# A two-layer backbone on one core: where the second attention's values, the output projection's weights and the last sums stand in the order

## The chip, the cores and the metric

The kernel runs on one core of a Trainium2 chip. A core has five engines with a queue of instructions each, and every queue runs in its order: TensorE (PE in the profile, with PEld for its weight loads), VectorE (DVE), ScalarE (ACT), GpSimd (POOL) and SyncE (SP), which starts most of the DMA transfers. Matmuls write to PSUM, which is divided into banks of 128 x 512 fp32. The metric is the time of one execution on the device in microseconds (us), as the median of several runs.

## The reference

512 latent tokens (`x`) and 256 context tokens (`ctx`) of width 1024 go through two layers, in fp32. Each layer is a mixer (an attention with its projections) and a SwiGLU FFN, both behind an RMSNorm with a shift and scale from a conditioning vector and followed by a gated residual. The heart of it:

```python
hx = _rms(x, norm_mix_w[l]) * (1.0 + scx1) + shx1          # same for ctx
if l % 2 == 0:   # 8 heads of windowed attention with a sink, 8 of dense attention, head size 64
    ax, ac = _even_mixer(hx, hc, ...)
else:            # 8 differential heads: two score maps of head size 64 on values of 128
    ax, ac = _odd_mixer(hx, hc, ...)
x = x + gx1 * ax
x = x + gx2 * _swiglu(_rms(x, norm_ffn_w[l]) * (1.0 + scx2) + shx2, ffn_w_in[l], ffn_w_out[l])
# ctx likewise, except in the last layer

def _diff_attend(q, k, v, lam):          # layer 1, one block of queries
    s = einsum('bqhad,bkhad->bhaqk', q, k) * scale
    p = softmax(s)
    a = p[:, :, 0] - lam * p[:, :, 1]
    return einsum('bhqk,bkhe->bqhe', a, v)      # then RMSNorm per head, then @ w_out

def _swiglu(h, w_in, w_out):             # hidden size 2816
    gate, up = split(h @ w_in)
    return (silu(gate) * up) @ w_out
```

## The kernel before

**Numbers.** Every large product is made of three matmuls on operands split in a high and a low part (`hi` is the value rounded by a copy on ACT, `lo` the rest by a subtraction): hi x hi, hi x lo and lo x hi. A weight takes this path too. `unit` starts a DMA into a raw tile, then ACT casts the high part (line 320, `woh`, `wgh`, `wuh` and so on) and either DVE (line 324) or POOL in four pieces (`sub_by_pool`, line 310) subtracts the low part (`wol`, `wgl`, ...).

**Tiles.** Tokens are in tiles of 128: 0 to 3 are latent, 4 and 5 context. The normalized input of a projection is kept transposed (`hT` for latent, `hTc` for context tokens, each hi and lo); a norm writes it by transposes on PE (`npt`, line 287), a scale and shift on ACT and DVE (lines 292 and 294) and a split (296 and 297). The sum of squares of a norm is taken on ACT (279), its inverse root on POOL (147, 148, then 281).

**Order.** Most of the order is not written out by hand: a scheduler walks the program, simulates it and puts each engine's instructions into one queue, by the order in which they are written, their priority (`tc.high_priority`) and when it holds their operands to be ready. Waits on a buffer come from pools: a tile with a tag gets one of the tag's buffers and waits until their last readers are done. A chip that is slower or faster than the simulation waits, but keeps the order.

**Layer 1's attention.** For head h of 8 and query tile t of 4 (line 1034), `attend1` makes scores (`sc`, 661 and 662), the maximum on DVE (664), exponentials on ACT (666), the difference of the two maps on DVE (673); then, behind a `yield`, transposes (`ppt`, 680), copies (`PT`, 683 and 685), the values (`av`, 688) and the norm per head (690 to 695). `Staggered` runs a step's first part, and then the rest of the step before it: values follow one step's scores. Queries and keys of the next head (`inps`, lines 421 to 423) come from a generator that `emit` advances between steps: a copy (`qkv`, 619), squares (`sq`, 375) and their sum (`qss`, 377), the inverse root (`rs_q`, 147 and 148), the scaled result (`qy`, 622), its split (`qd`, `kd`, 627 to 631), transposes (`qpt` 640, `kpt` 646) and their copies (`qt` 642, `kT` 647).

**Output projection.** `out_units` makes its eight weight K-tiles (tag `whi`/`wlo`, four buffers in each of two pools), for layer 1 with the third raw room `wor`. `OutProj.operand` writes a tile of attention results transposed into the place of `hT` (in layer 1 by transposes `opt`, then 728 and 729), `OutProj.sums` runs over the two halves n of 512 columns, and in each over the eight K-tiles (`ops`, 738 to 740), with the residual behind each half (`residual`: 428 multiplies by the gate, 429 adds). In layer 1 the weights are made at head 7, tile 0, and tiles 0 to 2 are projected between the steps of head 7; tile 3 and the four norms follow.

**FFN.** In eleven passes of two column blocks of 128, `pg` and `pu` (line 771) are gate and up sums in two PSUM tiles of the scores' pool `p_sc` (2 x 2 banks). Weights `wg`, `wu` use the same four buffers as the projection's weights. In the first pass the first block runs over two segments of tokens, so that it can start before all norms are there. The down sums (`dps`, 809 to 811) are made of one or two passes at once: nj = 2 blocks, or 4 at the end, where they take turns in two banks.

The lines around which the change works:

```python
ps = acc_tile("dps")                      # nj > 2: two banks, in turn
...
tag=("acc0", "tr0", "acc1", "tr1")[turn["sum"]]       # else: four banks
...
def push(self, gen):                      # Staggered
    next(gen)
    self.flush()
    self.last = gen
```

## Time and profile before

| | |
|---|---|
| median of 3 runs | 1806.88 us (1805.52 to 1808.76) |
| the profiled execution | 1809.33 us, span 1807.5 us |
| mean granted clock of TensorE | 0.986 |
| busy: PE, DVE, ACT, POOL | 1725.7, 995.7, 807.5, 618.6 us |
| moved by DMA | 165.65 MB, 92 GB/s |

The page lists for each engine how long it worked. A line of the waits says which instruction stood idle, and which other engine's instruction released it. A line of the timeline has the start, the length, the engine, the source line and the result's and operands' names; in square brackets how long the engine had been idle before, and what ended that. A granted clock of 0.50 means that TensorE ran at half its speed in that stretch.

The program's stages by time: layer 0's attention up to about 430 us, its FFN to 1020, the first projections of layer 1 to 1065, its attention to 1371, the rest of the output projection to 1419, the FFN to the end.

### The profile page before, as it was taken

What the parts mean: (1) busy time and instruction counts of PE and PEld (TensorE: products, weight loads), DVE (VectorE), ACT (ScalarE), POOL (GpSimd) and SP (SyncE); (2) the same over time, 40 slices, a digit from 0 to 9 for tenths busy, and PEclk for the clock granted to TensorE, in tenths of its full rate; (3) what the DMA queues carried; (4) which work ended last, traced back from release to release, by engine and by line L of the source; (5) the groups of instructions that cost most, each with busy time, mean ns of one, the idle gap of its engine ahead of it and who ended that gap; (6) DMA issues with size and microseconds to landing.
All of it is one profiled execution on the core that took longest, in us unless ns stands there. A gap on an engine that the chain in (4) does not pass through costs nothing. (4 is left out here: it accounts for less than half of the span.)

```text
span 1807.5 us, 26161 instructions
## 1 busy us (share of the span) xinstructions
PE 1725.7 (95%) x9910; PEld 1459.7 (81%) x9910; DVE 995.7 (55%) x1737; ACT 807.5 (45%) x1710; POOL 618.6 (34%) x944
## 2 busy tenths in 40 slices
PE   6899999889999999999999999999988999999998
PEld 4887787667888888888888889999977788888886
DVE  4665555435265465655552656666663556655653
ACT  6556556434264343333332566666663422232230
POOL 2763334322064344332322577776653100000000
PEclk8999999999999999999999999999999899999999
DMA  9212234203452334344331211111122233233231
GB/s 309 55 44 75 78 96 138 71 26 110 155 164 83 98 101 152 117 129 136 111 98 33 79 42 47 45 45 36 33 82 70 82 105 105 70 112 98 71 116 47
DMA packets 152478, 165.65 MB, mean 92 GB/s; under 512 B 16480, under 2 KB 139936, under 8 KB 152352
## 3 DMA queue, kind: packets, MB, share of 16 engines
q1 hardware_dynamic: 152000, 163.77, 29.1%
q8 instruction: 78, 1.28, 0.3%
q14 instruction: 48, 0.39, 0.1%
q10 hardware_dynamic: 352, 0.21, 0.0%
HBM read 159.73 MB, written 4.22 MB: 91 GB/s over the span
## 5 line engine op out<-in xcount | busy, mean ns | idle before, releaser
L771 PE MATMUL pg<-hT,wgh 128*128 128x512 f32 (+1 forms) x720 | 244.2, 391 | 0.8 <-DVE hT L297 0.7
L771 PE MATMUL pu<-hT,wuh 128*128 128x512 f32 (+1 forms) x720 | 243.6, 390 | 1.3 <-ACT wuh L320 1.3
L428 DVE TENSOR_TENSOR dps<-dps,g 128x512 f32<-128x512 f32 x200 | 136.2, 696 | 106.6 <-PE dps L811 99.3
L809 PE MATMUL dps<-wdh,hdh 128*128 128x512 f32 x440 | 175.9, 401 | 3.8 <-DVE x L429 3.5
L810 PE MATMUL dps<-wdl,hdh 128*128 128x512 f32 x440 | 174.1, 396 | 0.0
L811 PE MATMUL dps<-wdh,hdl 128*128 128x512 f32 x440 | 165.4, 395 | 0.0
L771 PEld LDWEIGHTS pg<-hT,wgh 128*128 128x128 f32 x720 | 135.3, 189 | 31.6 <-DVE hT L297 1.3
L771 PEld LDWEIGHTS pu<-hT,wuh 128*128 128x128 f32 x720 | 135.2, 189 | 31.0 <-ACT wuh L320 1.5
L771 PE MATMUL pu<-hT,wul 128*128 128x512 f32 (+1 forms) x360 | 140.4, 390 | 0.8 <-DVE wul L324 0.8
L771 PE MATMUL pg<-hT,wgl 128*128 128x512 f32 (+1 forms) x360 | 140.4, 390 | 0.0
L421 PE MATMUL inps<-wih,hT 128*128 128x384 f32 x384 | 133.2, 347 | 2.7 <-ACT qkv L619 2.7
L429 DVE TENSOR_TENSOR x<-x,dps 128x512 f32<-128x512 f32 x200 | 132.8, 683 | 3.3
L422 PE MATMUL inps<-wil,hT 128*128 128x384 f32 x384 | 130.6, 340 | 0.0
L423 PE MATMUL inps<-wih,hT 128*128 128x384 f32 x384 | 130.3, 339 | 0.0
L310 POOL TENSOR_TENSOR wil<-wir,wih 128x256 fp32r<-128x256 f32 x132 | 104.1, 817 | 69.7 <-ACT wih L320 69.1
L201 ACT ACTIVATE modw<-modw,cols 128x256 f32<-128x256 f32 x192 | 82.2, 498 | 82.8 <-DMA modw<-in_mod_w_dram 80.7
L434 ACT CAST hdh<-pu 128x768 fp32r<-128x768 f32 (+1 forms) x44 | 30.4, 691 | 177.6 <-DVE pu L787 177.6
L809 PEld LDWEIGHTS dps<-wdh,hdh 128*128 128x128 f32 x440 | 82.7, 188 | 26.0 <-DVE x L429 4.3
L771 PE MATMUL pg<-hTc,wgh 128*128 128x256 f32 x352 | 99.4, 286 | 2.3 <-ACT hTc L296 2.1
L811 PEld LDWEIGHTS dps<-wdh,hdl 128*128 128x128 f32 x440 | 82.3, 188 | 19.7
L771 PE MATMUL pu<-hTc,wuh 128*128 128x256 f32 x352 | 98.0, 282 | 0.0
L810 PEld LDWEIGHTS dps<-wdl,hdh 128*128 128x128 f32 x440 | 82.8, 188 | 17.9
(237 smaller groups left out, 4187.5 us busy)
## 6 DMA issues: line engine op xcount, KB each, us to landing
modw<-in_mod_w_dram SPq DMA_DIRECT2D x96, 512.0 KB, 4.9
wgr<-in_ffn_w_in_dram SPq DMA_DIRECT2D x44, 512.0 KB, 3.5
wur<-in_ffn_w_in_dram SPq DMA_DIRECT2D x44, 512.0 KB, 3.5
wdr<-in_ffn_w_out_dram SPq DMA_DIRECT2D x44, 512.0 KB, 3.5
wir<-in_od_w_in_dram SPq DMA_DIRECT2D x96, 128.0 KB, 2.3
x<-in_x_dram SPq DMA_DIRECT2D x8, 512.0 KB, 4.7
wir<-in_ev_w_in_dram SPq DMA_DIRECT2D x16, 256.0 KB, 3.0
wor<-in_ev_w_out_dram SPq DMA_DIRECT2D x8, 512.0 KB, 3.6
```

Source lines behind the costliest of these rows:

```text
L201: nc.scalar.activation(pr[:, k], w[:, k], AF.Copy, scale=cols[:, kk:kk + 1])
L310: nc.gpsimd.tensor_sub(lo[c], raw[c], hi[c])
L421: nc.tensor.matmul(ps, hs[0][:, k, :], a, start=k == 0, stop=False)
L422: nc.tensor.matmul(ps, hs[0][:, k, :], b, start=False, stop=False)
L423: nc.tensor.matmul(ps, hs[1][:, k, :], a, start=False, stop=k == KT - 1)
L428: nc.vector.tensor_mul(tmp, ps, g[:, n * 512:(n + 1) * 512])
L429: eng.tensor_add(xt[:, n * 512:(n + 1) * 512], xt[:, n * 512:(n + 1) * 512], tmp)
L434: nc.scalar.copy(hi, src)
L771: nc.tensor.matmul(ps[:, s0:s1], a, cols_T(b, s0, s1)[:, k, :], start=k == 0 and q == 0, stop=k == KT - 1 and q == 2)
L809: nc.tensor.matmul(ps, hh, a, start=j == 0, stop=False)
L810: nc.tensor.matmul(ps, hh, b, start=False, stop=False)
L811: nc.tensor.matmul(ps, hl, a, start=False, stop=j == nj - 1)
```

## The change

1. `Staggered` has a depth, in layer 1 two: values follow two steps' scores. `PBUF`, the buffers of the transposed probabilities, goes from 4 to 6. At the end the norms, the remaining values and the projection of tiles 2 and 3 are interleaved.
2. The weights of the output projections are made by `OutProj.weights` inside `behind_marks`: the last `qd` and `kd` and the last exponential on each engine are marked as they are written, and the weights are issued behind these. In layer 1 they begin at head 7, tile 1 instead of tile 0; in layer 0 three at block 3, tile 0 and the rest at tile 1.
3. `last_sums` makes the sums of the last projected tile (5 in layer 0, 3 in layer 1) K-tile by K-tile, both halves n in a tile of two banks, instead of half by half.
4. In layer 1's FFN `pg` and `pu` share one tile of two banks (`pgu`); the first pass runs both column blocks over two segments: 192 matmuls of 256 columns in place of 96 of 256 and 48 of 512.
5. The last down sums of layer 1 take turns in four banks, those of layer 0 do so for the first four sums.
6. `rt` is made by another form of instruction, 32 times.

```diff
-PBUF = 4
+PBUF = 6
...
+    def behind_marks():
+        stack = ExitStack()
+        for ins in marks.values():
+            stack.enter_context(tc.issue_after(ins))
+        return stack
...
-                nc.vector.tensor_sub(qd[:, 1], yb, f32(qd[:, 0]))
+                mark(nc.vector.tensor_sub(qd[:, 1], yb, f32(qd[:, 0])))
...
-            nc.scalar.copy(kd[:, :, 0, :], y[:, nq:nq + 2])
-            nc.gpsimd.tensor_sub(kd[:, :, 1, :], y[:, nq:nq + 2], f32(kd[:, :, 0, :]))
+            mark(nc.scalar.copy(kd[:, :, 0, :], y[:, nq:nq + 2]))
+            mark(nc.gpsimd.tensor_sub(kd[:, :, 1, :], y[:, nq:nq + 2], f32(kd[:, :, 0, :])))
...
+        def weights(self, n=KT):
+            with behind_marks():
+                self.ws.extend(w for _, w in zip(range(n), self.units))
...
+        def last_sums(self, t):
+            ohi, olo = tile_T(0, t), tile_T(1, t)
+            ps = p_sc.tile([P, 1024], F32, name="ops", tag="sc")
+            for k in range(KT):
+                for x, j, q in ((ohi, 0, 0), (ohi, 1, 1), (olo, 0, 2)):
+                    for n in range(2):
+                        c = slice(n * 512, (n + 1) * 512)
+                        nc.tensor.matmul(ps[:, c], x[:, k, :], self.ws[k][j][:, c],
+                                         start=k == 0 and q == 0, stop=k == KT - 1 and q == 2)
+            for n in range(2):
+                residual(self.xs[t], ps[:, n * 512:(n + 1) * 512], self.g[0 if t < NTX else 1], n)
...
+            def places():
+                if ntok > NTX:
+                    return [p_sc.tile([P, 1024], F32, name=name, tag="sc")[:, :n_tok] for name in ("pg", "pu")]
+                both = p_sc.tile([P, 1024], F32, name="pgu", tag="sc")
+                return both[:, :SEQ], both[:, SEQ:]
+
+            ps = []
+            if p == 0 and ntok == NTX:
+                ps = [places() for j in range(2)]
+                for s in first_segs:
+                    for j in range(2):
+                        for w, z in zip((wg, wu), ps[j]):
+                            half(j, w, z, [[s]])
...
+            sums = 0
...
-                    if nj > 2:
+                    sums += 1
+                    if nj > 2 and ntok > NTX and sums > 4:
                         ps = acc_tile("dps")
...
+                if b == 3 and t == 0:
+                    oproj.weights(3)
+                if b == 3 and t == 1 and hp == 0:
+                    oproj.weights()
...
-    for t in range(5, NT):
-        oproj.operand(t)
-        oproj.sums(t)
+    oproj.operand(5)
+    oproj.last_sums(5)
...
-            if h == 7 and t == 0:
+            if h == 7 and t == 1:
...
-            if h == 7 and 0 < t <= 3:
-                oproj.operand(t - 1)
+                oproj.weights()
+            if h == 7 and t >= 2:
+                oproj.operand(t - 2)
...
-                    oproj.sums(t - 1, 0, opa.pool, nc.gpsimd)
+                    oproj.sums(t - 2, 0, opa.pool, nc.gpsimd)
...
-    att.flush()
-    for t in range(3, NTX):
-        oproj.operand(t)
-        oproj.sums(t)
...
+    norm1(0)
+    att.pop()
+    oproj.operand(2)
+    with tc.high_priority(-1000):
+        oproj.sums(2, 0, opa.pool, nc.gpsimd)
+    norm1(1)
+    att.pop()
+    oproj.operand(3)
+    norm1(2)
+    oproj.last_sums(3)
+    norm1(3)
```

What this moves in the queues, at three places. Where lines above the change were added, the same statement has a higher line number after it (320 becomes 331, 310 becomes 321).

ACT in layer 1's attention, from the copy of the last projected query and key tile on. Before, `woh` are the casts of the first two weights, `sq` to `kd` the last query tile's chain:

```order
L619 COPY qkv<-inps 128x384
L320 CAST woh<-wor 128x1024 x2
L375 ACTIVATE sq<-qkv 128x256
L647 CAST kT<-kpt 128x2x128
L690 ACTIVATE o_9810<-av,rc 128x128
L642 CAST qt<-qpt 128x512
L693 ACTIVATE o_14027,oss<-o_9810 128x128
L627 CAST qd<-qy 128x256
L630 CAST kd<-qy 128x2x64
```

After:

```order
L630 COPY qkv<-inps 128x384
L386 ACTIVATE sq<-qkv 128x256
L658 CAST kT<-kpt 128x2x128
L701 ACTIVATE o_9808<-av,rc 128x128
L653 CAST qt<-qpt 128x512
L704 ACTIVATE o_13999,oss<-o_9808 128x128
L638 CAST qd<-qy 128x256
L641 CAST kd<-qy 128x2x64
L331 CAST woh<-wor 128x1024 x2
L658 CAST kT<-kpt 128x2x128
L653 CAST qt<-qpt 128x512
```

The two casts moved from behind `qkv` to behind the last `kd`, ahead of the copies of that tile's transposes.

POOL at the same place; before, `wol` is the first weight's subtraction in four pieces:

```order
L620 COPY vv<-qkv 128x128
L310 TENSOR_TENSOR wol<-wor,woh 128x256 x4
L147 TENSOR_SCALAR rs_o<-oss 128x1
L147 TENSOR_SCALAR rs_q<-qss 128x4
L148 TENSOR_TENSOR rs_o<-rs_o,neghalf 128x1
L148 TENSOR_TENSOR rs_q<-rs_q,neghalf 128x4
L622 TENSOR_TENSOR qy<-qy,rs_q 128x256
L631 TENSOR_TENSOR kd<-qy,kd 128x2x64
```

After:

```order
L631 COPY vv<-qkv 128x128
L158 TENSOR_SCALAR rs_q<-qss 128x4
L159 TENSOR_TENSOR rs_q<-rs_q,neghalf 128x4
L158 TENSOR_SCALAR rs_o<-oss 128x1
L633 TENSOR_TENSOR qy<-qy,rs_q 128x256
L159 TENSOR_TENSOR rs_o<-rs_o,neghalf 128x1
L642 TENSOR_TENSOR kd<-qy,kd 128x2x64
L321 TENSOR_TENSOR wol<-wor,woh 128x256 x8
```

The pieces moved from behind `vv` to behind `kd`, and are those of two weights there.

PE at the seam of the layers, around the transposes of the last latent tile's norm (`npt`) and of keys (`kpt`). Before:

```order
L287 MATMUL npt<-cst,nh 128x128 x8
L421 MATMUL inps<-wih,hT_110 128x384
L422 MATMUL inps<-wil,hT_110 128x384
L423 MATMUL inps<-wih,hT_111 128x384
L421 MATMUL inps<-wih,hT_110 128x384
L422 MATMUL inps<-wil,hT_110 128x384
L423 MATMUL inps<-wih,hT_111 128x384
L421 MATMUL inps<-wih,hTc_4716 128x256
L422 MATMUL inps<-wil,hTc_4716 128x256
L423 MATMUL inps<-wih,hTc_4717 128x256
L421 MATMUL inps<-wih,hTc_4716 128x256
L422 MATMUL inps<-wil,hTc_4716 128x256
```

After:

```order
L434 MATMUL inps<-wih,hT_111 128x384
L432 MATMUL inps<-wih,hT_110 128x384
L433 MATMUL inps<-wil,hT_110 128x384
L434 MATMUL inps<-wih,hT_111 128x384
L298 MATMUL npt<-cst,nh 128x128 x8
L657 MATMUL kpt<-identr,kd 128x128 x4
L432 MATMUL inps<-wih,hT_110 128x384
```

The twelve `inps` matmuls that stood between `npt` and `kpt` now stand ahead of `npt`.

## The prediction

> **What bounds the kernel now.** I read the page first, then the busy time by stage, then what TensorE waited for in the one stage where it is not busy, and last the order of time on each engine there.

> ```profile
> PE 1725.7 (95%) x9910; PEld 1459.7 (81%) x9910; DVE 995.7 (55%) x1737; ACT 807.5 (45%) x1710; POOL 618.6 (34%) x944
> ```

> TensorE (PE) is the bound: 1807.5 - 1725.7 = 81.8 us of idle time are all that a new order can win, besides time at a low granted clock. No other engine is near that. The stretches around the change, where the columns are the length, the busy time of PE, its weight loads, DVE, ACT and POOL, then the granted clock and the DMA share:

> ```profile
> 1065.00:1330.00 265.00, 258.73 (x1794) 247.69 (x1794) 176.40 (x349) 170.78 (x445) 175.13 (x314) 1.00 0.13 38
> 1330.00:1342.00 12.00, 5.14 (x30) 4.44 (x29) 4.34 (x8) 6.22 (x14) 8.35 (x13) 0.78 0.44 132
> 1342.00:1371.00 29.00, 24.05 (x133) 19.67 (x132) 21.55 (x34) 17.03 (x37) 12.94 (x18) 0.86 0.45 146
> 1371.00:1419.00 48.00, 47.18 (x235) 38.32 (x234) 15.65 (x27) 15.72 (x33) 15.40 (x21) 1.00 0.04 12
> 1419.00:1440.00 21.00, 17.47 (x105) 16.06 (x104) 14.51 (x24) 12.81 (x22) 1.85 (x3) 0.76 0.58 174
> 1440.00:1780.00 340.00, 340.00 (x1467) 273.73 (x1466) 192.19 (x246) 86.47 (x103) 0.00 (x0) 1.00 0.29 90
> ```

> The heads of layer 1 (265 us) lose 6.3 us, spread out. The attention's end and the weights of the output projection (1330 to 1371) lose 6.9 + 4.9 us, the projection itself 0.8, the start of layer 1's FFN 3.5. From 1440 to 1780 PE never stops: nothing to win there. The waits of PE from 1330 to 1440:

> ```profile
> PE qpt L640 <- ACT qd L627: 6.5, 1, 6.5
> PE ops L738 <- ACT hT L728: 2.5, 1, 2.5
> PE pu L771 <- ACT wuh L320: 1.3, 1, 1.3
> PE pu L771 <- DVE wul L324: 0.8, 1, 0.8
> PE npt L287 <- POOL nroom L281: 0.7, 1, 0.7
> PE pg L771 <- DVE hT L297: 0.7, 1, 0.7
> ```

> **The clock** costs time on top of the idle:

> ```profile
> 1364.00:1367.40 3.40, 2.35 (x7) 1.97 (x8) 3.12 (x7) 0.53 (x2) 1.66 (x2) 0.50 0.50 152
> ...
> 1422.00:1425.40 3.40, 1.62 (x11) 1.42 (x12) 1.96 (x3) 3.40 (x6) 0.76 (x3) 1.00 0.50 130
> 1425.40:1428.80 3.40, 2.71 (x13) 2.27 (x12) 3.05 (x4) 3.06 (x7) 1.09 (x1) 0.50 0.50 154
> 1428.80:1432.20 3.40, 2.73 (x13) 2.58 (x13) 2.56 (x6) 1.78 (x4) 0.00 (x0) 0.50 0.48 162
> 1432.20:1435.60 3.40, 3.40 (x18) 3.34 (x18) 1.87 (x3) 1.68 (x4) 0.00 (x0) 0.50 0.68 203
> ...
> 1029.50:1033.00 3.50, 2.53 (x18) 2.20 (x16) 2.29 (x6) 3.07 (x8) 0.00 (x0) 1.00 0.00 0
> ```

> A stretch of 3.4 us in which PE was busy for 1.62 us (48%) is followed by a clock of 0.50; one with 2.53 of 3.50 (72%) kept the full clock. At 0.50 half the busy time is lost: behind 1425.4 that is (2.71 + 2.73 + 3.40) / 2 = 4.4 us.

> **Weights behind the attention (layer 1).** In the order of time on ACT, POOL and ACT again:

> ```profile
> 1329.61 2.00 ACT L320 CAST woh<-wor 128x1024 fp32r<-128x1024 f32 x2
> 1331.51 0.42 ACT L375 ACTIVATE sq<-qkv 128x256 f32<-128x256 f32 x1
> ...
> 1330.74 3.94 POOL L310 TENSOR_TENSOR wol<-wor,woh 128x256 fp32r<-128x256 f32 x4 [0.42 <-ACT woh L320]
> 1335.83 1.01 POOL L148 TENSOR_TENSOR rs_q<-rs_q,neghalf 128x4 f32<-128x4 f32 x1
> 1336.92 0.61 POOL L622 TENSOR_TENSOR qy<-qy,rs_q 128x256 f32<-128x256 f32 x1
> ...
> 1337.56 0.40 ACT L627 CAST qd<-qy 128x256 fp32r<-128x256 f32 x1 [4.32 <-POOL qy L622]
> ...
> 1359.73 2.94 ACT L320 CAST woh<-wor 128x1024 fp32r<-128x1024 f32 x3 [1.17 <-DMA wor<-in_od_w_out_dram]
> ```

> The last query tile's normalization stands behind two weight casts (2.00) on ACT and one weight's subtraction (3.94) on POOL, and PE's 6.52 us is that queue. The change puts both behind. Then sq starts at 1329.6, when the casts do now, and about 4.5 us later (0.42, DVE's sum, 1.01, 0.61 and the gaps between) qd: PE can go on near 1334.5 instead of 1338.0, 3.5 us sooner. But the two casts now stand between kd and the copies of kT and qt, so the transposes behind those come only some 2.4 us sooner. What is late next are the weights: their last three casts waited for a DMA until 1359.73, and what a K-tile needs of POOL or DVE comes after that. From 1342 to 1371 DVE is busy for 21.55 of 29.00 us, so the chains of the last steps can't close up much. The 2.5 us wait at ops stays as likely as not. Ends: 0 (the weights hold the end as now) and -9.0 (6.5 + 2.5, both waits gone). I take **-2.5**, near the transposes' row, since a later part has not been shown to move.

> Two more outstanding steps of values give PE something to do in the heads; of 6.3 us, waits of some tenths each, I take **-0.5** (ends -2 and +2: deeper staggering also delays what frees the probabilities' buffers, six instead of four).

> The projection of the third token tile moves into the dense stretch with its norm; one more wait like that of npt (0.7): **+0.7** (-0.8, the idle there now, to +3).

> **Last sums by K-tiles; start of the FFN.** The FFN's first weights use the slots of the projection's:

> ```profile
> 1415.31 1.99 ACT L320 CAST wgh<-wgr 128x1024 fp32r<-128x1024 f32 x2
> ...
> 1421.93 1.04 ACT L320 CAST wuh<-wur 128x1024 fp32r<-128x1024 f32 x1 [3.62 <-DMA wur<-in_ffn_w_in_dram]
> ```

> Now the first half's eight K-tiles free no slot until the second half passes over them; by K-tiles the first four are free 24 matmuls before the last, and 24 matmuls of the FFN stand between. So the casts of wgh and wuh start earlier, and PE's waits for wuh and wul (1.3 + 0.8) go. That the last norm is late (npt 0.7, hT 0.7) is covered by the up half, which stands before it in the order. Of 3.5 idle and 4.4 of clock, 7.9 in all, 1.4 of idle may be left, and a stretch with 1.4 to 2 us of idle time is 41 to 59% idle: between the rows that halved and that which did not, so 0.5 us for a chance of 1 us at half clock. Taken: **-6.0** (ends -7.9 and -2.1: only the weights' waits go). [...]

> The 192 matmuls 256 wide (for 96 of them and 48 of 512) cost the columns they carry:

> ```profile
> 429.46 0.40 PE L738 MATMUL ops<-woh,hTc 128*128 128x512 f32 x1
> 429.69 0.40 PE L739 MATMUL ops<-wol,hTc 128*128 128x512 f32 x1
> ...
> 453.87 0.28 PE L771 MATMUL pg<-hTc,wgl 128*128 128x256 f32 x1
> 453.99 0.40 PE L771 MATMUL pg<-hTc,wgh 128*128 128x256 f32 x2
> ```

> 0.23 against 2 x 0.12 us: 48 x 0.01, at most 0.5, taken as 0.

> **Down sums, and the seam of the layers.** The waits of dps for a bank, the residual that frees it, and what stood at the seam (PE, PE, DVE; POOL, PE):

> ```profile
> 1785.89 0.50 PE L809 MATMUL dps<-wdh,hdh 128*128 128x512 f32 x1 [1.74 <-DVE x L429]
> 983.15 0.50 PE L809 MATMUL dps<-wdh,hdh 128*128 128x512 f32 x1 [1.74 <-DVE x L429]
> 981.22 1.30 DVE L428 TENSOR_TENSOR dps<-dps,g 128x512 f32<-128x512 f32 x2 [2.54 <-PE dps L811]
> ...
> 1033.49 0.52 POOL L620 COPY vv<-qkv 128x128 f32<-128x128 f32 x2 [4.56 <-DVE hT L297]
> 1034.35 0.44 PE L421 MATMUL inps<-wih,hT 128*128 128x384 f32 x1 [2.28 <-ACT qkv L619]
> ```

> At the end of layer 1 a third and fourth bank take the sums that now wait: **-1.7** (-1.7 to 0). In layer 0 three sums run ahead instead of two, and DVE does three products before the first addition, so the bank of the fifth sum comes one product (0.65) later: **+0.7** (-1.7 to +1).

> At the seam the order moves twelve inps matmuls from behind the last norm's transposes to before them. Behind these the next inps waits for copies that wait for that norm's hT. Twelve matmuls (six of 256 at the 0.12 us above, six of 384 at 1.5 times that: 1.8 us) no longer cover the chain; PE waits 4.1 instead of 2.28. So +1.8, and +0.8 for about an even chance of one stretch at half the clock (1.7): **+2.6** (0, if the earlier dps bring the norm forward by as much, to +5.2 with two such stretches).

> ```profile
> 427.95 0.50 PE L738 MATMUL ops<-woh,hTc 128*128 128x512 f32 x1 [1.51 <-DVE x L429]
> 448.88 0.39 PE L771 MATMUL pg<-hTc,wgh 128*128 128x256 f32 x1 [2.12 <-ACT hTc L296]
> ```

> At the end of layer 0's attention the last sums by K-tiles take the 1.51 away, but the last context norm behind them comes no sooner (both halves end together, and its transposes stand behind the 48 pg and pu matmuls), so the 2.12 grows by that: **0** (-1.5 to +1). The weights of layer 0 move by some casts inside dense work: 0. rt stays 32 instructions on one column: 0.

> Sum: -2.5 - 0.5 + 0.7 - 6.0 - 1.7 + 0.7 + 2.6 = **-6.7 us**. The profiled execution took 1809.33 us, 2.45 above the median of 1806.88, so it is an ordinary one; against the median that gives 1800.2, against its own time 1802.6.

> **Rivals.**
> - *The half clock goes as well (more gain).* The stretch at 1364 is halved behind the wait of 2.5; should that shrink to less than half a stretch, the two from 1364.0 (2.35 busy, then 3.40 at most) give back 2.9, and the wait 2.5, the seam staying as it was (-2.6): -6.7 - 8.0 = -14.7, 1792.2. For it: the clock follows idle. Against it: DVE's 21.55 of 29.00.
> - *The wait moves (no change).* What the queues no longer hold, the weights do: the attention's end gives 0, and the FFN's start only 2.1 + half its clock (2.2), -4.3. Then -0.5 + 0.7 - 4.3 - 1.7 + 0.7 + 2.6 = -2.5, 1804.4. For it: the casts at 1359.73 that wait for DMA.
> - *The weights come too late (slower).* All weights wait for the last kd and exponentials; the last of them are needed by the first projection's second four K-tiles, with no work behind. Each microsecond past 1364 is one of PE. Without the attention's gain the sum is -4.2; slower by 0.2% needs +7.8 there: the last casts near 1367.5 instead of 1359.7. At 10 us late: 1806.9 - 4.2 + 10 = 1812.7. Against it: the casts of the first pair start only some 5 us later than now.

> **Numbers.** A timing of this kernel can tell about 0.2% (3.6 us) from no change; the three runs span 3.2 us. Forecast 0.46 (own range 1796 to 1803.2), more gain 0.24, the wait moves 0.19, too late 0.11. Faster 0.70, same 0.19, slower 0.11. The range of 1788 to 1808 holds the first three and leaves out the late weights and the tail of more gain.

> **What would show it.** Right: the wait of qpt for qd under 3 us; none of pu for wuh; clock near 1 in the 20 us at the FFN's start; no wait of dps in the last 30 us; the inps behind the last npt of the seam waiting over 4 us. Wrong: waits of ops for woh or wol of several microseconds, a clock of 0.5 for two stretches more at the seam, or the heads of layer 1 longer than 265 us.

## The result and the profile after

The changed kernel takes **1822.64 us** (median of 4 runs, 1818.92 to 1823.97) against 1807.03 for the kernel before (1805.52 to 1808.76): 1.0083 times as long, with an interval of 1.0064 to 1.0101. The forecast was 1800.2 and its range ended at 1808, so both the sign and the size were wrong. The profiled execution took 1823.74 us, 14.4 more than that of before.

TensorE's line on the page, and then the stretches that lie around the seam of the layers and around the end of layer 1's attention (length, busy time of PE, its weight loads, DVE, ACT and POOL, granted clock, DMA share, GB/s). After:

```profile
PE 1731.4 (95%) x9958; PEld 1464.8 (80%) x9958; DVE 992.6 (54%) x1737; ACT 809.5 (44%) x1710; POOL 616.5 (34%) x944
...
975.00:1065.00 90.00, 77.54 (x409) 67.83 (x408) 47.06 (x97) 42.04 (x92) 51.35 (x85) 0.91 0.21 64
1347.00:1387.00 40.00, 30.03 (x155) 24.57 (x155) 21.62 (x36) 20.61 (x45) 15.11 (x21) 0.82 0.41 131
1435.00:1462.00 27.00, 22.49 (x140) 20.68 (x139) 12.14 (x20) 9.97 (x17) 1.86 (x3) 0.87 0.35 98
1462.00:1790.00 328.00, 328.00 (x1440) 265.20 (x1440) 189.81 (x246) 86.72 (x103) 0.00 (x0) 1.00 0.31 93
```

The seam in the kernel before, whose row was not read for the prediction:

```profile
975.00:1065.00 90.00, 82.49 (x459) 72.98 (x459) 49.71 (x103) 45.12 (x101) 55.58 (x91) 0.96 0.21 64
```

In the 90 us at the seam PE is busy 5 us less than before, at a lower clock (0.50 for 17.1 us of them, against 6.8 before), and gets 50 matmuls less done. In the 40 us from 1347 it stands still for 10 us, at a clock of 0.82; in the 29 us of the kernel before that correspond to the most of them it stood still for 4.9. The dense FFN is as it was: no idle time at all.

A row of time does not say by itself which work was late. So I aligned the traces: for each moment of the kernel before I added up the columns that TensorE had streamed by then, and looked up when the other kernel had streamed as many. The differences of two such moments are what a kernel loses or gains in a stage. In us, other kernel minus before (one profiled execution each, so good to some 2 us; stages in the time of the kernel before):

| stage | forecast | after | e1 | e2 | e3 | e5 | e6 | e13 | e9 |
|---|---|---|---|---|---|---|---|---|---|
| up to 975: layer 0 | 0 | -0.6 | -1.7 | -2.9 | +0.1 | -4.0 | +0.1 | -3.8 | -2.0 |
| 975 to 1100: seam, first head | +3.3 | **+10.7** | +6.8 | +11.2 | +10.0 | +4.6 | +8.8 | +0.3 | +2.1 |
| 1100 to 1325: heads | -0.5 | -0.8 | -1.1 | -0.8 | -0.4 | -0.6 | +1.9 | -0.2 | -0.2 |
| 1325 to 1371: attention's end, weights | -2.5 | **+5.5** | -0.6 | -2.5 | -2.4 | +3.5 | +0.4 | -3.3 | -2.7 |
| 1371 to 1475: projection, start of the FFN | -5.3 | **+1.9** | +1.2 | -1.2 | +2.0 | +0.4 | 0.0 | +2.6 | -0.9 |
| 1475 to 1800: the rest of the FFN | -1.7 | -2.5 | -2.7 | -2.5 | -2.5 | -2.5 | -0.9 | -2.5 | -2.5 |

The columns e1 to e13 are experiments told below: e1 and e6 concern layer 0's four banks, e2 the marks, e3 the second step, e5 layer 0's banks and the marks on its weights; e13 and e9 are repaired versions. Three stages of the changed kernel went otherwise than forecast.

**The seam.** What TensorE waited for from 975 to 1065 us (us in total, times, longest), after:

```profile
PE inps L432 <- ACT qkv L630: 3.0, 2, 2.5
PE inps L433 <- POOL wil L321: 3.0, 2, 2.8
PE dps L849 <- DVE x L440: 2.7, 1, 2.7
PE kpt L657 <- ACT nhc L303: 2.1, 1, 2.1
PE qpt L651 <- DVE qd L639: 1.2, 1, 1.2
```

The same view before:

```profile
PE inps L421 <- ACT qkv L619: 2.5, 2, 2.3
PE inps L422 <- POOL wil L310: 2.5, 2, 1.7
PE dps L809 <- DVE x L429: 1.7, 1, 1.7
PE qpt L640 <- DVE qd L628: 0.4, 1, 0.4
```

The wait of kpt is new, that of dps is 1.0 longer, and the later ones for wil and qd grew too (wil's longest from 1.7 to 2.8, its sum from 2.5 to 3.0). Two places of PE's order of time show how they come in two pairs (start, length, and in brackets the wait):

```profile
1035.64 0.79 PE L657 MATMUL kpt<-identr,kd 128*128 128x128 f32 x4 [2.11 <-ACT nhc L303]
1038.95 0.69 PE L432 MATMUL inps<-wih,hT 128*128 128x384 f32 x1 [2.52 <-ACT qkv L630]
...
1054.63 0.36 PE L651 MATMUL qpt<-identr,qd 128*128 128x128 f32 x2 [1.22 <-DVE qd L639]
1059.54 0.58 PE L433 MATMUL inps<-wil,hTc 128*128 128x256 f32 x1 [2.76 <-POOL wil L321]
```

Behind each pair the clock is at half for 6.8 us, from 1037.1 and from 1057.6 (length, PE's and the other engines' busy time, clock):

```profile
1036.50:1045.00 8.50, 6.05 (x22) 6.05 (x23) 4.75 (x13) 3.53 (x10) 5.53 (x11) 0.60 0.01 2
1056.90:1065.00 8.10, 5.00 (x24) 4.70 (x25) 1.33 (x3) 2.31 (x6) 7.40 (x14) 0.58 0.45 128
```

**The end of the attention.** The wait of qpt for the last query tile did shrink, from 6.5 to 2.4; the wait of ops for hT grew from 2.5 to 6.8. The waits of PE from 1330 to 1470 us:

```profile
PE ops L751 <- ACT hT L741: 6.8, 4, 3.8
PE qpt L651 <- ACT qd L638: 2.4, 1, 2.4
PE pgu L795 <- DVE x L440: 2.4, 1, 2.4
PE ppt L691 <- DVE hT L742: 2.0, 2, 1.0
...
PE gps L251 <- ACT nroom L303: 1.3, 1, 1.3
...
PE pgu L795 <- ACT hT L307: 0.7, 1, 0.7
```

hT, the operand of the projection, is itself held up on ACT, behind the casts of the last three weights, which wait for their DMA. ACT's order of time:

```profile
1374.13 2.94 ACT L331 CAST woh<-wor 128x1024 fp32r<-128x1024 f32 x3 [3.96 <-DMA wor<-in_od_w_out_dram]
1376.98 1.06 ACT L741 CAST hT<-opt 128x512 fp32r<-128x512 f32 x2
```

**The start of the FFN.** The waits for wuh and wul are gone, as forecast. In their place the first up sums (pgu) wait 2.4 us for a residual x, in the list above, and gps and pgu wait once more for the last norm: 4.4 us in all where the kernel before lost 3.5.

### The profile page after: what moved, and what is told of

It reads as the page before. It is cut to its first block, busy times and chain, and to the rows that moved or that the text cites. A ratio compares the mean times of both kernels' runs of the same rounds, so it can differ in the third digit from the quotient of the medians.

```text
span 1822.0 us, 26253 instructions
## 1 busy us (share of the span) xinstructions
PE 1731.4 (95%) x9958; PEld 1464.8 (80%) x9958; DVE 992.6 (54%) x1737; ACT 809.5 (44%) x1710; POOL 616.5 (34%) x944
## 5 line engine op out<-in xcount | busy, mean ns | idle before, releaser
L795 PE MATMUL pu<-hT,wuh 128*128 128x512 f32 x352 | 129.5, 391 | 0.6 <-DVE x L440 0.6
L795 PE MATMUL pg<-hT,wgh 128*128 128x512 f32 x352 | 129.8, 392 | 0.0
L795 PE MATMUL pgu<-hT,wgh 128*128 128x512 f32 (+1 forms) x384 | 115.6, 384 | 3.3 <-DVE x L440 2.4
L795 PE MATMUL pgu<-hT,wuh 128*128 128x512 f32 (+1 forms) x384 | 113.6, 376 | 0.0
L331 ACT CAST wgh<-wgr 128x1024 fp32r<-128x1024 f32 x44 | 46.1, 1049 | 115.4 <-PE pgu L795 70.6
L335 DVE TENSOR_TENSOR wgl<-wgr,wgh 128x1024 fp32r<-128x1024 f32 x44 | 54.4, 1240 | 75.7 <-ACT wgh L331 75.7
L213 POOL TENSOR_TENSOR modw<-modw 128x512 f32<-128x512 f32 x48 | 63.1, 1314 | 84.0 <-ACT modw L212 78.8
```

The costliest lines, as they stand in the source:

```text
L213: nc.gpsimd.tensor_add(pr[:, 0:2], pr[:, 0:2], pr[:, 2:4])
L795: nc.tensor.matmul(ps[:, s0:s1], a, cols_T(b, s0, s1)[:, k, :], start=k == 0 and q == 0, stop=k == KT - 1 and q == 2)
```

## The experiments

Each kernel is timed beside the kernel before, whose median over all these runs is 1806.6 to 1806.8 us. Diffs are against the kernel that the text names.

**e1: layer 0's last down sums in two banks as before; all else as changed.**

```
-                    if nj > 2 and ntok > NTX and sums > 4:
+                    if nj > 2 and ntok > NTX:
```

> The changed kernel, with the last down sums of layer 0 in two banks again. Against the kernel before, aligned by work done on TensorE, the changed one loses about 2 us at the first of these sums and 8.6 us more at the seam of the layers. If the four banks of these sums are the cause (they run ahead, and the norm's transposes and inps change places), this kernel gains 8 to 11 us on the changed one: 1812 to 1815. Rival: the seam is ordered by what comes after it (deeper staggering, later weights), or by waits that the banks have no part in; then it stays at 1820 to 1824, and the two stretches at half clock near 1037 and 1057 stay.

1812.23 us (1810.49 to 1817.14), 1.0033 times before (1.0020 to 1.0046): 10.4 less than the changed kernel. The edit that was priced at +0.7 takes two thirds of the loss with it. In its trace 3.9 of that lie at the seam and 6.1 at the attention's end (table), 300 us after the edit: the order of the instructions differs there too. At the seam 6.8 us stay: the longer wait of dps and the one of kpt are gone, but the second pair (1.2 for qd, 2.4 for wil) is there without the banks as well. ACT in e1 has the operand hT ahead of the last three weights' casts, the changed kernel behind them:

```profile
1365.12 0.59 ACT L741 CAST hT<-opt 128x512 fp32r<-128x512 f32 x1 [1.89 <-PE opt L740]
1367.41 2.94 ACT L331 CAST woh<-wor 128x1024 fp32r<-128x1024 f32 x3 [1.71 <-DMA wor<-in_od_w_out_dram]
```

**e2: the changed kernel without the marks**, so that no weight waits for the attention's chains.

```
-        for ins in marks.values():
-            stack.enter_context(tc.issue_after(ins))
```

> The changed kernel, without the marks: the weights of both output projections may be issued as soon as the scheduler sees fit, still from head 7, tile 1 on in layer 1. If issuing behind the marks makes the last weights of layer 1 late (the last cast ran 14.4 us later than before, at 1374.1 against 1359.7), it gains 6 to 10 us: 1812 to 1816. Rival: not the marks but the opening one tile later (rooms of the pools closed there) makes the weights late; then it stays within 2 us of 1822 and the last three casts still start past 1370, and the wait of ops for hT of 3.8 us stays.

1814.14 (1809.64 to 1816.13), 1.0035 (1.0021 to 1.0049): 8.5 less than the changed kernel.

**e3: the changed kernel with values one step behind**, four buffers for the probabilities, and layer 1's weights opened, and the first three tiles projected, one step earlier, as before; the weights stay behind the marks.

```
-PBUF = 6
+PBUF = 4
...
-    att = Staggered(2)
+    att = Staggered(1)
...
-            if h == 7 and t == 1:
+            if h == 7 and t == 0:
```

> The changed kernel with values behind one step's scores in layer 1 (as before), four buffers of probabilities, and the weights opened at tile 0 of head 7, still behind the marks. If the later opening makes the weights late, it gains 6 to 10 us: 1812 to 1816, the last casts before 1365. If the marks do, it stays at 1818 to 1824. The heads of layer 1 (about 260 us) become some 1 us longer than in the changed kernel if the second step pays at all.

1815.16 (1810.91 to 1816.80), 1.0042 (1.0028 to 1.0056): 7.5 less. In the table e2 and e3 take the same loss away: the +5.5 at the attention's end becomes -2.5 and -2.4, and the seam's stays at +11.2 and +10.0. So neither the marks nor the second step costs that alone. Nor are both enough: e1 has both and loses nothing there. The time is the one expected for a late opening, but its sign, last casts before 1365, is not there, and e10 below shows the opening to cost nothing. With one step, as in e1, hT stands ahead of the last three casts on ACT. In e3:

```profile
1371.18 0.59 ACT L741 CAST hT<-opt 128x512 fp32r<-128x512 f32 x1 [0.36 <-PE opt L740]
1371.95 2.94 ACT L331 CAST woh<-wor 128x1024 fp32r<-128x1024 f32 x3 [0.18 <-DMA wor<-in_od_w_out_dram]
```

**e4: the kernel before with four banks at the end of layer 1 alone.**

```
-                    if nj > 2:
+                    if nj > 2 and ntok > NTX:
```

> The kernel before, with only layer 1's last down sums in four banks. The wait of 1.74 us for a bank at 1784 goes, and the whole gains 1.7 to 2.4 us, 1804.5 to 1805.3. Rival: the bank's wait is only moved to another wait of the same end (the last hidden block's split); then within 0.5 us of the kernel before.

1806.62 (1800.61 to 1809.86), 0.9991 (0.9979 to 1.0004). The wait of dps at the end is not gone in its trace, only shorter, 1.40 us instead of 1.74:

```profile
1789.89 0.50 PE L809 MATMUL dps<-wdh,hdh 128*128 128x512 f32 x1 [1.40 <-DVE x L429]
```

By the medians that moves nothing, by the ratio -1.6 us, which the interval can't tell from zero.

**e5: the changed kernel with layer 0 left as it was** (two banks there, its output weights loaded at once and unmarked; its last sums by K-tiles stay).

```
-                    if nj > 2 and ntok > NTX and sums > 4:
+                    if nj > 2 and ntok > NTX:
...
+            oproj.ws.extend(oproj.units)
...
-                if b == 3 and t == 0:
-                    oproj.weights(3)
-                if b == 3 and t == 1 and hp == 0:
-                    oproj.weights()
```

> The changed kernel with the last down sums of layer 0 in two banks and the weights of layer 0 issued at once, as before; layer 1 as changed (two steps, marks, last sums by K-tiles, shared gate and up tile, four banks at the end). In this kernel the queues at the seam (from the last down sums to the first heads) stand nearly as before. If the loss is the order of the queues at the seam, this kernel loses nothing there and the changes of layer 1 show alone: 1803 to 1807. Rival: the tail of layer 1 by itself costs what the aligned traces show in the changed kernel (8 us from 1325 to 1420): 1811 or more.

1811.40 (1808.22 to 1817.47), 1.0030 (1.0017 to 1.0043). Taking back the marks on layer 0's weights as well is worth little beside e1; 4.7 us stay, as its rival expected. In its trace they lie at the seam and first head (+4.6) and at the attention's end (+3.5), where hT again stands behind the last casts, less 4.0 in layer 0.

**e6: the kernel before with the four banks of both layers**, the other side of e1.

```
+            sums = 0
...
-                    if nj > 2:
+                    sums += 1
+                    if nj > 2 and ntok > NTX and sums > 4:
```

> The kernel before, with the last down sums in four banks as in the change (layer 1 all, layer 0 the first four), nothing else. If these banks alone reorder the seam, it loses there what the first experiment gave back, less 2 us at the end: 1812 to 1816, with a wait of dps of 2.7 us near 985 and the stretch from 1020 to 1100 some 8 us longer. Rival: the seam needs the other changes too, and it is 1804 to 1807.

1815.44 (1812.89 to 1819.54), 1.0053 (1.0037 to 1.0069): 8.7 more than before, and what layer 1's banks gain (e4) has to be added. Nothing else of the change is in this kernel, and its waits from 975 to 1065 are those of the changed kernel:

```profile
PE inps L421 <- ACT qkv L619: 2.7, 2, 2.3
PE dps L811 <- DVE x L429: 2.7, 1, 2.7
PE inps L422 <- POOL wil L310: 2.4, 1, 2.4
PE kpt L646 <- ACT nhc L292: 2.1, 1, 2.1
PE qpt L640 <- DVE qd L628: 1.2, 1, 1.2
```

So layer 0's four banks are enough for the seam's loss, and they move the order there (kpt behind npt, with the twelve inps ahead) by themselves. All five kernels with these banks (the changed one, e2, e3, e6, e14) have the waits of 2.7 for dps and 2.1 for kpt, and none of the others has. Whether the banks would cost anything with the order as before was not tried, since the order follows from them.

**e7: e5 with one step**, so that layer 0 is as in e5 and values as before; marks on layer 1's weights, last sums by K-tiles and layer 1's four banks stay. The edit is that of e3 on e5.

> As the kernel with the seam as before, but values behind one step's scores and the weights of layer 1 opened at tile 0 of head 7, behind the marks. Against that kernel it tells what the second step is worth. If the second step and the later opening cost at the attention's end, this one is 1 to 4 us faster than it; if the second step pays in the heads (0.9 us of waits there), 1 us slower. Then 1801 to 1808.

1805.94 (1801.47 to 1809.32), 0.9997 (0.9985 to 1.0009): 5.5 less than e5, and 9.2 less than e3, which differs from it in layer 0 alone. Without layer 0's banks and marks and without the second step the loss is gone, but there is no gain either.

**e8: the kernel before with layer 0's output weights behind the marks.** Added: the marks on the attention's chains, the function for the weights, and in layer 0

```
+                if b == 3 and t == 0:
+                    oproj.weights(3)
+                if b == 3 and t == 1 and hp == 0:
+                    oproj.weights()
```

> The kernel before, with only layer 0's projection weights issued behind the marks, at the changed kernel's places. In the queues this moves casts and subtractions at the end of layer 0's attention and little behind it. If the marks of layer 0 cost by themselves (the changed kernel loses 2.2 us from 200 to 400 us, aligned by work), 1808 to 1811. Rival: those casts lie beside dense work, and the difference from 200 to 400 was that of one execution: 1805.5 to 1808.

1809.47 (1804.59 to 1814.41), 1.0016 (1.0004 to 1.0028): about +2.8, with its own runs 9.8 us apart. Its trace loses 3.1 us between 300 and 450, as the changed kernel does between 300 and 400 (2.8). In the aligned traces all five kernels with these marks (the changed one, e1, e3, e8, e14) lose some 3 us between 300 and 350, and no other loses 1; in e8 the scores (sc) there wait 4.8 us for copies on ACT instead of 2.4.

**e9: e7 with layer 1's last sums by K-tiles in the accumulators' two banks** instead of one of the two tiles that the scores, and later pgu, use.

```
-            ps = p_sc.tile([P, 1024], F32, name="ops", tag="sc")
+            if self.l:
+                ps = [acc_tile("ops", one=n) for n in (1, 0)]
+            else:
+                both = p_sc.tile([P, 1024], F32, name="ops", tag="sc")
+                ps = [both[:, :512], both[:, 512:]]
```

> As the kernel with the seam as before and one step, but layer 1's sums of the last token tile are in the two banks that its other sums used, not in a tile of the scores' pool. In the changed kernel and in all its variants the first gate and up matmuls of the second column block wait 2.1 to 3.1 us for DVE's addition of x (line 440), the reader of the last sums' tile, since the pool has two tiles. If that is the cause, this wait goes, and with it half clock behind it: 2 to 5 us less than the kernel it is made from (1805.9), 1801 to 1804. Rival: the waiting place needs the last norm, not the tile; then the wait stays above 1.5 us and the time at 1805 to 1807.

1801.33 (1799.37 to 1803.41), **0.9967 (0.9954 to 0.9979)**: 4.6 less than e7 and faster than both kernels. pgu no longer waits for a residual. The waits of PE from 1415 to 1460:

```profile
PE gps L251 <- ACT nroom L303: 1.5, 1, 1.5
PE npt L298 <- POOL nroom L292: 0.8, 1, 0.8
PE pgu L799 <- ACT hT L307: 0.7, 1, 0.7
```

**e10: e7 with layer 1's weights opened in the second step of the last head**, as the changed kernel has it, and the first projection's sums with them.

```
-            if h == 7 and t == 0:
+            if h == 7 and t == 1:
                 wp.close()
...
+            if h == 7 and t == 1:
+                oproj.operand(0)
+                with tc.high_priority(-1000):
+                    oproj.sums(0, 0, opa.pool, nc.gpsimd)
             if h == 7 and t >= 2:
```

> As the kernel with the seam as before and one step, but layer 1's projection weights are opened at tile 1 of head 7 instead of tile 0, as in the changed kernel. With two steps (and the opening at tile 1) the time was 1811.4, with one (at tile 0) 1805.9. If the later opening makes the difference, this kernel is at 1810 to 1812; if the second step does, at 1805 to 1807.

1805.80 (1803.24 to 1809.97), 0.9994 (0.9985 to 1.0003): the same as e7. The later opening by itself costs nothing.

**e11: e7 without the marks** (the edit of e2; layer 0's output weights are also written in its last block, as in the changed kernel, three and then five).

> As the kernel with the seam as before and one step, but without marks in layer 1 (the weights of layer 0 behind none either, three issued at tile 0 and five at tile 1 of the last block). If the marks are what takes the wait of qpt for qd from 6.5 to 2.4 us, it comes back, and the kernel is 3 to 4 us slower: 1808.5 to 1810. Rival: what the marks win there the later weights give back, 1805 to 1807.

1808.15 (1805.81 to 1810.45), 1.0003 (0.9994 to 1.0012): 2.2 more than e7 by the medians, between the two expectations, and the intervals overlap. The wait of qpt for qd is back at 6.5.

**e12: the kernel before with the marks on layer 1's weights and layer 1's four banks, nothing else.** Of the marks the short form:

```
+        with behind_marks():
+            self.ws.extend(w for _, w in zip(range(n), self.units))
...
-                    if nj > 2:
+                    if nj > 2 and ntok > NTX:
```

> The kernel before, with two parts of the change alone: layer 1's projection weights behind the marks, and layer 1's last down sums in four banks. If the marks in layer 1 are worth the 3.4 us that the aligned trace shows by 1340 and the banks 1.6, and the FFN's new start is a loss, this kernel beats both: 1801 to 1804. Rival: the weights come late and give the marks' gain back at ops, 1805 to 1808.

1801.71 (1801.19 to 1804.86), **0.9973 (0.9961 to 0.9984)**. It differs from e4 in the marks alone (and in that the weights are written behind the gate's row), and is 3.3 us faster by the ratios, 4.9 by the medians: with one step the marks gain, by about what the forecast gave them (-2.5). It matches e9, which has the last sums by K-tiles, the shared tile and the other edits of layer 1 besides: with the tile in the accumulators these together cost nothing, and gain nothing that these runs can tell.

**e13: e7 with the six buffers of the changed kernel (PBUF 6)**, since the step and the buffers had been taken back together.

> As e7 (layer 0's last down sums in two banks, its output weights loaded at once, values one step behind, layer 1's output weights opened in the last head's first step), but with the six buffers of the probabilities that the change has (PBUF 6 instead of 4). e7 took 1805.9 us, e5 with two steps, six buffers and the opening in the second step 1811.4; the opening alone cost nothing (e10, 1805.8). Theory 1, the second outstanding step of values costs the 5.5 us itself: 1806 (1804 to 1808), and the third and fourth raw weight's DMAs wait under 1 us for a product av, as in e7. Theory 2, the two more buffers cost it, since they move what lies behind them in memory: 1811 (1809 to 1813), and the DMA's wait of 5 us for an av is back.

1804.48 (1802.62 to 1808.24), 0.9991 (0.9982 to 1.0000). The buffers cost nothing; the second step (with the opening, which cost nothing in e10) is what e5 has and e13 has not, 6.9 us. In the table 6.8 go at the attention's end (+3.5 against -3.3) and 4.3 at the seam and in the first head, and 2.2 come back at the FFN's start.

**e14: the changed kernel with the last sums' tile of e9.**

> The changed kernel with one line of work moved: layer 1's last sums by K-tiles go to the two banks of the accumulators instead of one of the two tiles of the scores' pool. Changed kernel 1822.6 us. Theory 1, the scores' tile is what the FFN's first sums wait for in the changed kernel too (a wait of 2.38 us for the residual at 1446 us, half clock behind): 1818 (1816 to 1820), no wait of pgu for the residual x at the FFN's start. Theory 2, in the changed kernel the late weights hold that stage, so that the bank is not what counts: 1822 (1820.5 to 1824), with waits of the same length for hT, nroom or weights there.

1820.33 (1818.80 to 1824.55), 1.0078 (1.0064 to 1.0091), so 2.3 less than the changed kernel, between the two expectations and with overlapping intervals. The wait for x goes, as in e9, but others take its place, from 1425 to 1470:

```profile
PE npt L298 <- POOL nroom L292: 2.1, 1, 2.1
PE gps L251 <- ACT nroom L303: 1.5, 1, 1.5
PE pgu L799 <- ACT hT L307: 0.6, 1, 0.6
```

That is 4.2 us against 4.4. In the changed kernel the chain of the last norm is as late as the bank, so that freeing the bank shows the norm.

## Why the prediction was wrong, step by step

**Down sums of layer 0 and the seam: +0.7 and +2.6 forecast, +10.7 in the aligned traces, 8.7 for the banks alone (e6).** This is the step that cost most. The wait of dps went nearly as reckoned, one product later (1.74 to 2.7), but the clock fell to half behind it (0.50 for 3.4 us from 985.9). The wait of the inps behind the last norm was also sized rightly: 4.1 forecast, 2.11 + 2.52 = 4.6 measured, in two waits. The step failed in stopping there. The same order puts the last projected tiles' chain and the weights' casts and subtractions later, and the next two waits, for qd and wil, grew from 0.4 and 1.7 to 1.2 and 2.8 (in e6, with the banks alone, to 1.2 and 2.4; e1 has them without the banks, so that is not their only way). I had looked at the order of PE at one place and priced one wait; POOL's and ACT's order in the following 20 us was not followed, though the prediction's own rule was to ask what is late next. And the clock was charged with 0.8, about half a stretch of 3.4 us, where three stretches more were at half: 17.1 us against 6.8.

**Weights behind the attention and the heads: -2.5 and -0.5 forecast, +5.5 and -0.8 measured.** The mechanism of the marks was right: qpt waits 2.4 instead of 6.5, the gain of 4.1 against 3.5 forecast, and with one step the marks are worth 3.3 (e12 against e4), near the -2.5. What failed is that the second step was priced in the heads alone (as "two more" steps, where it is one more), and its part in the end was not priced at all. Two things got late there. First the weights: SP's queue shows the DMA of a raw weight waiting for a product av, in the changed kernel

```profile
SPq L327 <- PE av L699: 5.0, 1, 5.0
```

a row that e3 and e13 do not have. It is not the second step's alone: e1, with two steps, lacks it too, and e11, with one and no marks, waits 3.9 so. Second the operand hT, which comes a step later and stands behind those weights on ACT, so that PE waits for both. The second decides more than the first. The last casts start at 1374.1 in the changed kernel and at 1367.4 in e1; less the 9.3 and 4.0 us by which these programs are behind at 1325, that is 1364.8 and 1363.4, against 1359.7 before. Nearly equally late weights, then, but e1, with hT ahead of them, loses nothing and the changed kernel 5.5. That the loss needs both the marks and the second step is shown by e2 and e3, that it is neither the opening nor the buffers by e10 and e13; and e1 shows that both are not enough. That hT's place on ACT is what decides is read from the traces of e1, e3 and e13 (ahead, no loss) beside those of e5, e14 and the changed kernel (behind, +3.0 to +5.5); no kernel moved it by itself. It needs late weights with it: in the kernel before, in e10 and in e11 hT stands behind them too, with the last casts at 1359.7, 1362.4 and 1357.6 and nothing lost (e10: -0.9). What sets hT's place in the scheduler's order stays open.

The rival "the weights come too late" (1812.7, chance 0.11) has a part of this: it named the last casts, of whose 14.4 us only some 5 arise here. Its argument against itself, that the first pair starts only some 5 us later, looked at the first casts and not at the room that the later ones need.

The first head is open in part. Between 1065 and 1100, e5, e14 and the changed kernel, all with two steps, and e3, with one, lose some 2 to 3 us, e1 and e2, with two steps, some 1, e13, e9 and e6 at most 0.4. The first four are those whose clock is at 0.50 for one more stretch of 3.4 us, from 1085.5 in e5 and from 1097 to 1101 in the others; that is up to 1.6 of it. The rest is idle time, most of it waits for the weights wil and wih (1.7 for wil in the changed kernel). Why these come late in kernels with so different edits was not found.

**Last sums by K-tiles and the start of the FFN: -6.0 forecast (-5.3 with the dense projection), +1.9 measured.** The waits for wuh and wul went, as the step said. It overlooked what the new tile does besides holding sums: there are two tiles in that pool, pgu needs one as soon as the sums end, and the residual has to read it first. The stage from 1371 to 1475 of the kernel before and the same work in the changed kernel and in e9:

```profile
1371.00:1475.00 104.00, 99.65 (x496) 82.91 (x495) 49.13 (x75) 37.61 (x66) 17.26 (x24) 0.95 0.23 71
```

```profile
1385.80:1491.70 105.90, 99.09 (x542) 83.84 (x541) 49.35 (x75) 37.56 (x65) 18.44 (x24) 0.97 0.24 70
```

```profile
1368.24:1471.37 103.13, 96.87 (x536) 81.63 (x535) 48.97 (x76) 35.93 (x61) 18.62 (x26) 0.98 0.27 82
```

Even with the tile moved away this work takes 0.9 less than before, not 5.3: 1.4 of idle time were to be left, and e9 has 6.3, counting the projection in front. The term was too large by itself; the norm's chain, which the prediction held to be covered by the up half, takes 3.0 in e9 (gps, npt and pgu above). And 4.4 of the 7.9 us that the term could win were half clock in one execution. e8 has this stage as the kernel before has it, with 4.9 us of idle time, and the clock does not fall:

```profile
1419.00:1440.00 21.00, 16.08 (x120) 14.22 (x119) 14.57 (x24) 13.42 (x23) 1.86 (x3) 1.00 0.56 175
```

The part on the clock below shows idle time at the seam that was not followed by 0.50 either.

**Four banks at the end of layer 1: -1.7 forecast, -2.5 in the aligned traces**, and no wait of PE at all is left from 1475 on. The size came out, but not by the banks alone. With them and the old gate and up tiles (e4, e6, e12) the stage gains 0.9 and the last dps still waits 1.40; the wait is gone only in kernels that also have `pgu`, for which the forecast had nothing. That `pgu` is what takes the rest was not tried by itself.

**Layer 0's attention: 0 forecast.** Its marked weights cost about 2.8 (e8). In the first row of the table this is hidden: there e5, e13 and e9, whose layer 0 is the same, already differ by 2 us. The cover was named, dense work, and was not checked against the queues that the marks put the weights in.

**The clock.** The prediction read two rows as a rule: a stretch busy for 48% halves the clock, one busy for 72% does not. What it lacked is where the stretches lie. In each of the sixteen traces the changes of the clock are whole multiples of 3.413 us apart (in those of before and after, from 100 to 1800 us, to about 1 ns). I cut the time into stretches of that length, as these changes lie; a wait falls into one of them or across two. The wait of inps at the seam is 2.28 us before and 2.27 in e7, with the same order of work around it. Before, it lies from 1032.07 to 1034.35, across two stretches, which are busy for 75 and 57%, and the clock stays at full. In e7 it lies from 1030.28 to 1032.55, nearly all in one, which is busy for 37%, and the next is at half. Before, then e7:

```profile
1029.48:1032.89 3.41, 2.55 (x19) 2.22 (x16) 2.20 (x6) 2.96 (x8) 0.00 (x0) 1.00 0.00 0
1032.89:1036.31 3.42, 1.96 (x11) 1.97 (x12) 2.52 (x8) 1.96 (x6) 1.86 (x6) 1.00 0.02 5
1036.31:1039.72 3.41, 3.41 (x22) 3.41 (x21) 1.89 (x7) 1.48 (x4) 3.25 (x6) 1.00 0.00 0
```

```profile
1028.96:1032.37 3.41, 1.27 (x10) 0.94 (x9) 1.64 (x3) 2.76 (x7) 0.53 (x2) 1.00 0.00 0
1032.37:1035.78 3.41, 3.23 (x10) 3.23 (x11) 3.05 (x10) 1.33 (x4) 2.45 (x6) 0.50 0.02 5
```

So in the execution where two stretches shared this wait no fall of the clock followed, and in the one where nearly all of it was in one stretch 3.4 us at 0.50 did; one profile's half clock is not a price that an edit can count on winning.

**The rivals and the shares.** The loss of 15.6 us is, by stages, +10.7 at the seam and in the first head and +5.5 at the attention's end, with small terms of both signs elsewhere. Taking back single edits gives back 10.4 (e1), 8.5 (e2) and 7.5 (e3), more than there is, since each of the three also mends the attention's end. Of the signs that the prediction named, the waits of qpt, of wuh and of dps at the end came as for its being right, and the half clock at the seam as for its being wrong; the clock near 1 at the FFN's start did not come (0.87). The case that came true, the seam, was none of the rivals. Its upper end was in the working (+5.2 with two half stretches, against +2.6 taken), but the range gave no chance to one edit's order being worse at several places at once.

## What to carry to other kernels

When an edit changes how many banks or tiles a group of sums may hold, compare the order of every engine from there to the end, not only around the wait that the edit was made for: here that wait grew by 1 us, and the order that came with it cost nine. Before work is put into a pool's tile, ask who takes the next one; e9 moved one tile to another pool and was worth 4.6 us. Two edits that are harmless alone (weights behind the chains, values a step later) may meet in one engine's queue, so try them apart first: e12, with two small parts of the change, was as fast as anything else here.

## What the runs showed of the hardware

What 0.50 costs: in e7 matmuls of 384 columns start 0.17 us apart at full clock (1028.10, 1028.27) and 0.32 at 0.50 (1033.03, 1033.35, 1033.67). By these, 3.4 us at 0.50 cost about 1.6 us, an estimate, where the prediction took half, 1.7.

The scalar product rt on one column took a median of 273 ns written as a tensor-scalar operation, and 220 as a scalar-tensor-tensor one, though it reads the same two scalars (ns, least, median and most; before and then after):

```profile
L672 DVE SCALAR_TENSOR_TENSOR rt<-sm,nlam,rc x32: 204/220/225, 1067.0 to 1365.6; 128x1 f32<-128x1 f32 x32
```

```profile
L683 DVE TENSOR_SCALAR rt<-sm,nlam,rc x32: 272/273/276, 1070.8 to 1368.5; 128x1 f32<-128x1 f32 x32
```

That is 32 x 0.05 = 1.7 us of DVE, which no wait of PE in these traces shows.
